# A two-layer decoder trunk on one core: output weights fetched two steps before they are split, and four pieces of work moved in the order

## The chip, the core and the metric

The kernel runs on one NeuronCore of a Trainium2 chip. The metric is device time of one launch in microseconds. PE is TensorE, DVE is VectorE, ACT is ScalarE, POOL is GpSimd, SP is SyncE, whose queue issues the DMAs.

## The reference, cut to what matters

```python
def mixer_sublayer(x, mem, w_in, w_mem_kv, w_out, main_fn):
    h = x @ w_in                       # columns [main | mem q | main gate | mem gate]
    y_main = main_fn(u_main)           # layer 0: causal pooling; layer 1: forgetting attention
    y_mem = memory_attention(q_mem, mem, w_mem_kv)      # 4 heads into 256 memory tokens
    y = concatenate([y_main * silu(g_main), y_mem * silu(g_mem)])
    return y @ w_out                   # then layer_norm(ALPHA * x + y)

def forgetting_attention(u, k, v, cum):                 # 16 heads of 64, causal
    logits = q @ k.T / 8 + cum[t] - cum[s]              # cum: running sum of log forget gates
    return softmax(logits) @ v
```

x is 1024 x 1024 in float32, there are two layers, and keys, values and forget gates of the second are projected once from the output of the first.

## The kernel before, in words

Every projection keeps float32 accuracy by splitting each operand into a rounded high part and a low remainder (`hi_lo`: ACT casts the high part, L142, DVE subtracts the low part, L143; `gp_hi_lo` does both on POOL, L146 and L147) and adding three products. A `slab` (L181) is one 128-column projection of all 1024 tokens: 48 matmuls with 512 columns each, two weight loads from `raw` buffers (three of them, shared by all weight loads), two evictions.

The order of PE is written out by hand. A `Fill` object holds generators of slab matmuls, and `pump(cols)` issues so many columns of them between the pieces of attention, so that PE has work while DVE and ACT do the softmax. DVE, ACT, POOL and SP are ordered by the scheduler.

**Memory attention** (`mem_attention`, once in each layer) loops over t = 0 to 9. For t < 8 `probs(t)` computes the logits of 128 tokens, their softmax (L283 to L294 on DVE and ACT) and a transposing DMA. At t = 3, 5, 7, 9 `values(c, h)` runs for four heads h; each is 12 matmuls into the only buffer of the tag O, taken out by DVE (L310). The fill is four gate slabs, spread evenly: one part behind the logits and one behind each h, at t = 9 three parts and then half parts.

**Start of the forgetting attention** (`start_units`): values and forget logits of the first heads (`v_first`), the first pair's keys and queries (`own`), a chain of small DVE operations for the forget gates, then their cumulative sum over tokens (L605 and L607 on PE), its transpose (L611), eight DMAs into `cumd` (L615) and the first loads of R, a row of `cumd` broadcast to all partitions (L670). `following` is the second pair's work: a key slab and a query slab.

**Forgetting attention** (`fox`): 8 pairs of heads, 16 steps in each pair (8 token tiles for each head, the longest first). A step computes the logits of one tile (L169 into the tag L, two buffers), DVE adds R and takes the minimum (L689), ACT exponentiates (L695) and scales (L712), DVE forms the remainder (L713), SP issues a transposing DMA (L722), and five steps later the values follow (L169 into O, evicted by L738 and L739). The pair's fill is spread evenly over its steps: three slabs (keys, queries, values) of the next pair, with evictions L627, L628, L638, L639 and, for the values, L651 and L236 to L244, and gate slabs of `gate_ahead` (L194, L195). Gates 0 and 1 run in pair 0, 2 in pair 2, 4 in pair 4, 7 in pair 7. Gates 3, 5 and 6 are late: their attention output goes to DRAM ungated, and in pair 7 `late_gate` reads it back into an R buffer, multiplies (L756, POOL) and writes it again; the others are multiplied in `pair_out` (L748, POOL).

**Output projection** (`OutProj`): W_out comes as 24 half tiles of 256 KB. `load` (L343) issues a transfer and the two split operations of `hi_lo` in one go, one half tile a step from the start of pair 7, eight in all; the rest follow in `rest`. `early` loads the memory part of y for the first 256 tokens and splits it, and its 48 matmuls fill the last five steps (L358).

Of the kernel before, what the change touches and what calls it, by code (L numbers as in the profile page):

```python
# [15 lines left out]
ALU = mybir.AluOpType  # L16
AX = mybir.AxisListType

P = 128
# [3 lines left out]
ST = S // P  # L23
# [48 lines left out]
def trunk_kernel(ctx, tc, x, xT, memT, win, wk, wv0, wv, wmk, wmv, wout, poolw, pscale, lng, lnb, bforget, out):  # L72
# [186 lines left out]
    def mem_attention(l, XH, XL, kv, qtile, ytile, yd):  # L259
# [52 lines left out]
        with tc.manual_schedule(engines={PE}):  # L312
            for t in range(ST + 2):
                part = fill.left / (5 * (ST + 2 - t))
                if t < ST:
                    probs(t)
                fill.pump(part if t <= ST else 3 * part)
                for h in range(MH):
                    if t >= 3 and t % 2 == 1:
                        values((t - 3) // 2, h)  # L320
                    fill.pump(part if t <= ST else part / 2)
            fill.pump(float("inf"))
        for h in range(MH):
            nc.vector.tensor_tensor(ys[h], ys[h], gs[h], ALU.mult)  # L324
# [2 lines left out]
    class OutProj:  # L327
# [2 lines left out]
        KKS = (4, 5, 0, 1, 2, 3)  # L330

        def __init__(self, l, wtile, yd):
            self.l, self.wtile, self.yd, self.ws, self.accs, self.n = l, wtile, yd, [{}, {}], None, 0

        def load(self, upto):

            for n in range(self.n, upto):
# [4 lines left out]
                r = raw([P, NH])  # L342
                nc.sync.dma_start(r, wout[self.l, nh, 2 * kk + j])  # L343
                hi_lo(h[j], lo[j], r)
            self.n = max(self.n, upto)

        def open(self, banks=(("pj", 3),) * 2 + (("L", 2),) * 2):
            accs = [ps([P, NH], *bank) for bank in banks]
# [12 lines left out]
                            )  # L361
                            yield NH

        def early(self, tiles):

            yh, yl = tiles
            for j in range(2):
                r, two = raw([P, 2, 2 * P]), slice(2 * j, 2 * j + 2)
                nc.sync.dma_start(r, self.yd[2, :, two, : 2 * P])
                hi_lo(yh[:, two, :], yl[:, two, :], r)  # L370

            def units():
                self.accs = self.open()
                yield from self.products(self.accs, 2, yh, yl)

            return units()

        def rest(self, resid, XH, XL, dst):
            self.load(24)
# [138 lines left out]
    with tc.tile_pool(name="in1", bufs=1) as in1:  # L518
# [135 lines left out]
        def start_units(own, following):  # L654

            yield from islice(own, 48)
            yield from v_first()
            gates = forget_gates()
            next(gates)
            for _ in v_turned():  # L660
                yield from islice(own, 6)
            yield from own
            next(gates)
            yield from islice(following, 9)
            next(gates)
            yield from islice(following, 39)

        def forget_rows(hd):
            R = sb([P, S], "R", 2, F32, in1)
# [1 line left out]
            return R  # L671

        def probs(hd, i, R, sums, behind):

# [77 lines left out]
        def late_gate(pr):  # L752
            o, g = sb([P, S], "R", 2, F32, in1), G()
            nc.sync.dma_start(o, y1d[pr // 4, :, pr % 4, :])
            yield from gate_units(win[1, 12 + pr], g, XH, XL)
            nc.gpsimd.tensor_tensor(o, o, g, ALU.mult)  # L756
            nc.sync.dma_start(y1d[pr // 4, :, pr % 4, :], o)

        def fox(following, out_proj):
# [8 lines left out]
            for hd in range(HEADS + 1):  # L768
# [3 lines left out]
                if hd < HEADS:  # L772
                    if b == 0:
                        o, sums = G(), sb([P, 4 * ST], "sums", 2, F32, small).rearrange("p (n b i) -> p n b i", n=2, b=2)
                        if 0 < pr < 7:
                            fill.add(pair_units(pr + 1), 3 * SLAB)
                        for ahead in {0: (0, 1), 2: (2,), 4: (4,), 7: (7,)}.get(pr, ()):
                            gate_ahead(ahead)
                        if pr == 0:
                            fill.add(following, SLAB)  # L780
                        for late in (3, 5, 6) if pr == 7 else ():
                            fill.add(late_gate(late), SLAB)
                    R, ahead_R = ahead_R, None
                for i in range(ST if hd < HEADS else LAG):
# [11 lines left out]
                        ahead_R = forget_rows(hd + 1)  # L796
                    if pr == 7:
                        step = b * ST + i
                        out_proj.load(min(step + 1, 6) if step < 9 else 8)
                        if step == 6:  # L800
                            lead = out_proj.early([xy((P, 4, 2 * P)) for _ in range(2)])
                    if hd < HEADS:
                        new = (hd, tile_of, o)
                        fresh[0] = probs(hd, tile_of, R, sums, behind)
# [85 lines left out]
```

## Time and profile before

| | us |
|---|---|
| three runs | 1282.02, 1282.96, 1287.71 |
| median | 1282.96 |
| profiled execution, its own time | 1289.07 |
| its span, first to last instruction | 1287.3 |
| PE busy / DVE / ACT / POOL | 1251.9 / 801.4 / 579.2 / 168.8 |
| mean granted TensorE clock | 0.993 |

A busy figure is the time in which an engine had an instruction under way; matmuls overlap, so a busy PE may still run slowly. Windows are stretches of the span, and a window's line gives each engine's busy time with the number of instructions, the granted clock (1.00 is full) and the DMA engines' busy share. In a timeline a bracket gives the idle time ahead of a group and what ended it. The profiled execution is one of several, and its times are some microseconds above the median's.

### The profile page before, as it was taken

To read this page: it belongs to the slowest core of one execution; us is meant where nothing else is said; L and a number is where in the kernel's file an instruction comes from. 1 tells how busy PE (TensorE), PEld (TensorE's weight loads), DVE (VectorE), ACT (ScalarE), POOL (GpSimd) and SP (SyncE) were. 2 spreads that over 40 slices of the span, in tenths; PEclk is the share of its full clock that TensorE was granted. 3 is DMA by queue.
4 is the path that set the end of the run, shared out by engine and by line. 5 is a ranking of instruction groups with operands and counts; after the bars stand their busy time and mean duration, and the time that the engine had idled before them with its cause. 6 is when DMAs were issued, how large, how long until landed. Compare 5 with 4: busy or idle time off the path is not lost. (4 is left out here: it accounts for less than half of the span.)

```text
span 1287.3 us, 19678 instructions
## 1 busy us (share of the span) xinstructions
PE 1251.9 (97%) x7018; PEld 1036.6 (81%) x7018; DVE 801.4 (62%) x1905; ACT 579.2 (45%) x1273; POOL 168.8 (13%) x267
## 2 busy tenths in 40 slices
PE   9999999999999999999999999999999999999997
PEld 7888878888778889887887788887888777788885
DVE  6452656355565457267456777777777887674644
ACT  5332642232331124265225667766766776653110
POOL 0000000000000000000003334333334231420000
PEclk9999999999999999999999999999999999999999
DMA  6351343212474226234516866868778786986430
GB/s 221 115 148 50 92 98 114 82 56 91 158 243 137 92 91 183 64 82 112 169 47 157 160 153 162 192 143 172 171 163 185 164 187 155 230 200 200 164 115 33
DMA packets 267426, 178.65 MB, mean 139 GB/s; under 512 B 212288, under 2 KB 225728, under 8 KB 267328
## 3 DMA queue, kind: packets, MB, share of 16 engines
q1 hardware_dynamic: 267328, 177.40, 52.0%
q8 instruction: 55, 0.90, 0.3%
q14 instruction: 43, 0.35, 0.1%
HBM read 94.97 MB, written 22.61 MB: 91 GB/s over the span
## 5 line engine op out<-in xcount | busy, mean ns | idle before, releaser
L181 PE MATMUL pj<-A,w 128*128 128x512 f32 x2928 | 726.5, 396 | 1.0 <-POOL w L147 0.6
L181 PEld LDWEIGHTS pj<-A,w 128*128 128x128 f32 x2928 | 539.5, 189 | 105.8 <-ACT A L142 1.8
L143 DVE TENSOR_TENSOR w<-raw,w 128x512 fp32r<-128x512 f32 x106 | 72.9, 689 | 117.0 <-ACT w L142 115.5
L142 ACT CAST w<-raw 128x512 fp32r<-128x512 f32 x106 | 65.6, 621 | 162.4 <-PE pj L181 103.7
L695 ACT ACTIVATE T<-MK,s 128x512 f32<-128x512 f32 x192 | 110.8, 577 | 56.6 <-DVE s L689 43.3
L713 DVE SCALAR_TENSOR_TENSOR P<-T,s,P 128x512 f16<-128x512 f32 x192 | 111.5, 613 | 34.5 <-ACT P L712 32.9
L712 ACT ACTIVATE P<-T,s 128x512 f16<-128x512 f32 x192 | 102.6, 576 | 48.2 <-issue 20.9
L169 PE MATMUL L<-B,B 128*128 128x512 f32 (+3 forms) x384 | 93.1, 346 | 13.9 <-DVE s L689 11.6
L169 PEld LDWEIGHTS L<-B,B 128*128 128x128 f32 x384 | 70.0, 188 | 36.2 <-DVE s L689 20.9
L689 DVE CUSTOM_DVE_ANT_0 MK<-L,R 128x512 f32<-128x512 f32 (+3 forms) x128 | 72.9, 570 | 15.9 <-PE L L169 10.7
L601 POOL MEMSET G<- 128x128 f32 x1 | 0.2, 205 | 620.3 <-DVE V L324 620.3
L169 PEld LDWEIGHTS <-V 128*128 128x128 f16 x1152 | 65.9, 99 | 17.9 <-issue 17.4
L169 PE MATMUL O<-T,V 128*128 128x128 f16 x1152 | 77.0, 222 | 0.0
L147 POOL TENSOR_TENSOR w<-raw,w 128x512 fp32r<-128x512 f32 x54 | 69.8, 1292 | 3.9
L142 ACT CAST T<-T 128x1024 fp32r<-128x1024 f32 x23 | 24.2, 1051 | 93.4 <-DMA T<-y1d 49.3
L682 POOL TENSOR_SCALAR_AFFINE_SELECT R<-R 128x128 f32<-128x128 f32 x128 | 40.4, 318 | 190.4 <-DVE s L689 107.7
L143 DVE TENSOR_TENSOR T<-T,T 128x1024 fp32r<-128x1024 f32 x23 | 28.1, 1220 | 58.1 <-PE L L358 41.6
L146 POOL TENSOR_SCALAR w<-raw 128x512 fp32r<-128x512 f32 x54 | 36.4, 675 | 143.6 <-PE pj L181 131.7
L213 PE MATMUL pj<-T,w 128*128 128x256 f32 x384 | 48.9, 285 | 2.7 <-ACT w L142 2.1
L213 PEld LDWEIGHTS pj<-T,w 128*128 128x128 f32 x384 | 46.9, 191 | 4.3 <-ACT w L142 2.8
L358 PE MATMUL pj<-B,T 128*128 128x512 f32 x186 | 46.5, 392 | 0.8 <-DVE B L143 0.8
L358 PE MATMUL L<-B,T 128*128 128x512 f32 x174 | 42.5, 389 | 0.0
(212 smaller groups left out, 1599.9 us busy)
## 6 DMA issues: line engine op xcount, KB each, us to landing
raw<-in_win_dram SPq DMA_DIRECT2D x96, 256.0 KB, 2.7
raw<-in_wout_dram SPq DMA_DIRECT2D x48, 256.0 KB, 3.3
B<-B SPq DMA_DIRECT2D x32, 256.0 KB, 3.9
R<-cumd SPq DMA_DIRECT2D x16, 512.0 KB, 4.3
y0d<-Y SPq DMA_DIRECT2D x12, 512.0 KB, 2.7
T<-y0d SPq DMA_DIRECT2D x12, 512.0 KB, 4.3
T<-y1d SPq DMA_DIRECT2D x11, 512.0 KB, 4.5
raw<-in_wmk_dram SPq DMA_DIRECT2D x16, 256.0 KB, 2.7
```

Source lines behind the costliest of these rows:

```text
L142: nc.scalar.copy(hi, src)
L143: nc.vector.tensor_tensor(lo, src, hi.bitcast(F32), ALU.subtract)
L147: nc.gpsimd.tensor_tensor(lo, src, hi.bitcast(F32), ALU.subtract)
L169: nc.tensor.matmul(acc, a, b, start=i == 0, stop=i == len(terms) - 1)
L181: nc.tensor.matmul(accs[n], a[:, k, :], b[:, kt, n * NH : (n + 1) * NH], start=kt == 0 and i == 0, stop=kt == KT - 1 and i == 2,)
L213: nc.tensor.matmul(acc, w[:, k, :], m[pc][:, k, :], start=pc == 0 and k == 0 and i == 0, stop=pc == 1 and k == 3 and i == 2,)
L358: nc.tensor.matmul(accs[a][nh], y[:, k, a * P : (a + 1) * P], w, start=kt == 8 and i == 0, stop=kt == 7 and i == 2,)
L682: nc.gpsimd.affine_select(R[:, qs], R[:, qs], [[-1, P]], ALU.is_ge, -NEG, base=0, channel_multiplier=1)
L689: nc.vector.tensor_tensor_reduce(p[:, lo:up], lg, R[:, lo:up], 1.0, top, ALU.add, ALU.min, m[:, n : n + 1])
L695: nc.scalar.activation(e, p[:, lo:up], AF.Exp, bias=top, scale=-1.0, accum_out=sums[:, n, hd % 2, i : i + 1],)
L712: nc.scalar.activation(pair[:, lo:up], e, AF.Copy, scale=r)
L713: nc.vector.scalar_tensor_tensor(pair[:, L + lo : L + up], e, r, pair[:, lo:up], ALU.mult, ALU.subtract)
```

## The change

Six edits in one:

- In `mem_attention`, at each t, three parts of the fill go behind the logits and half a part behind each head.
- `load` becomes `fetch`, which issues the transfer only, and `split`, which runs `hi_lo` on what was fetched. In pair 7, tile n is fetched in one step and split two steps later; the last two are split in steps 14 and 15.
- `early` becomes a generator whose two loads and two splits are issued in steps 7, 9, 10 and 12.
- In `start_units`, nine matmuls of `following` go ahead of the cumulative sum, and nine fewer go behind the transpose.
- In `fox`, gate 3 is filled in pair 3, no longer late; in pair 0 the rest of `following` (the second pair's queries) stands between gate 0 and gate 1.
- `late_gate` multiplies in four column pieces.

```diff
-                fill.pump(part if t <= ST else 3 * part)
+                fill.pump(3 * part)
                 for h in range(MH):
                     if t >= 3 and t % 2 == 1:
                         values((t - 3) // 2, h)
-                    fill.pump(part if t <= ST else part / 2)
+                    fill.pump(part / 2)
...
-        def load(self, upto):
+        def fetch(self, upto):
+            while self.n + len(self.raws) < upto:
+                n = self.n + len(self.raws)
+                r = raw([P, NH])
+                nc.sync.dma_start(r, wout[self.l, n // 2 % 2, 2 * self.KKS[n // 4] + n % 2])
+                self.raws.append(r)
+        def split(self, upto):
+            while self.n < upto:
+                self.fetch(self.n + 1)
...
+                hi_lo(h[j], lo[j], self.raws.pop(0))
+                self.n += 1
...
         def early(self, yh, yl):
             for j in range(2):
                 r, two = raw([P, 2, 2 * P]), slice(2 * j, 2 * j + 2)
                 nc.sync.dma_start(r, self.yd[2, :, two, : 2 * P])
+                yield
                 hi_lo(yh[:, two, :], yl[:, two, :], r)
+                yield
+            self.accs = self.open()
+            yield from self.products(self.accs, 2, yh, yl)
...
             yield from own
+            yield from islice(following, 9)
             next(gates)
             yield from islice(following, 9)
             next(gates)
-            yield from islice(following, 39)
+            yield from islice(following, 30)
...
-            nc.gpsimd.tensor_tensor(o, o, g, ALU.mult)
+            for c in range(4):
+                cols = slice(c * 2 * P, (c + 1) * 2 * P)
+                nc.gpsimd.tensor_tensor(o[:, cols], o[:, cols], g[:, cols], ALU.mult)
...
-                        for ahead in {0: (0, 1), 2: (2,), 4: (4,), 7: (7,)}.get(pr, ()):
+                        for ahead in {0: (0, 1), 2: (2,), 3: (3,), 4: (4,), 7: (7,)}.get(pr, ()):
                             gate_ahead(ahead)
-                        if pr == 0:
-                            fill.add(following, SLAB)
-                        for late in (3, 5, 6) if pr == 7 else ():
+                            if ahead == 0:
+                                fill.add(following, SLAB)
+                        for late in (5, 6) if pr == 7 else ():
                             fill.add(late_gate(late), SLAB)
...
-                        out_proj.load(min(step + 1, 6) if step < 9 else 8)
-                        if step == 6:
-                            lead = out_proj.early([xy((P, 4, 2 * P)) for _ in range(2)])
+                        if step == 7:
+                            lead = out_proj.early(*(xy((P, 4, 2 * P)) for _ in range(2)))
+                        if step in (7, 9, 10, 12):
+                            next(lead)
+                        out_proj.split(min(step - 1, 6) if step < 14 else step - 7)
+                        out_proj.fetch(min(step + 1, 6) if step < 12 else min(step - 5, 8))
```

More of the change, by code (lines that the diff above doesn't have):

```diff
@@ L332, in __init__ @@
         def __init__(self, l, wtile, yd):
-            self.l, self.wtile, self.yd, self.ws, self.accs, self.n = l, wtile, yd, [{}, {}], None, 0
-        def load(self, upto):
-            for n in range(self.n, upto):
+            self.l, self.wtile, self.yd, self.ws, self.accs = l, wtile, yd, [{}, {}], None
+            self.raws, self.n = [], 0
+        def fetch(self, upto):
[7 more added lines that the diff above has]
+                self.fetch(self.n + 1)
+                n = self.n
                 kk, nh, j = self.KKS[n // 4], n // 2 % 2, n % 2
@@ L341, in load @@
                 h, lo = self.ws[nh][kk]
[L342 to L345, printed above, removed]
+                hi_lo(h[j], lo[j], self.raws.pop(0))
+                self.n += 1
         def open(self, banks=(("pj", 3),) * 2 + (("L", 2),) * 2):
@@ L362, in products, with early @@
                             yield NH
-        def early(self, tiles):
-            yh, yl = tiles
+        def early(self, yh, yl):
             for j in range(2):
@@ L369, in early @@
                 nc.sync.dma_start(r, self.yd[2, :, two, : 2 * P])
+                yield
                 hi_lo(yh[:, two, :], yl[:, two, :], r)
[L372 to L376, printed above, removed]
+                yield
+            self.accs = self.open()
+            yield from self.products(self.accs, 2, yh, yl)
         def rest(self, resid, XH, XL, dst):
-            self.load(24)
+            self.split(24)
             gb = []
```

## The prediction

> **What bounds the kernel now.** I read the busy line of the page first, then the windows of the eight attention pairs, then the timeline of PE and DVE at each place where PE stood, and last the granted clock around those places.
>
> ```profile
> PE 1251.9 (97%) x7018; PEld 1036.6 (81%) x7018; DVE 801.4 (62%) x1905; ACT 579.2 (45%) x1273; POOL 168.8 (13%) x267
> ```
>
> PE is the bound: 1287.3 - 1251.9 leaves 35 us. No edit changes the number of matmuls, so only PE's waits, and what the waits bring with them, can move the time. A 512-column matmul follows the next one at 0.227 us (24 of L358 take 5.44 us in the chain).
>
> The next lines are windows from the first logits of a pair to those of the next: PE, PEld, DVE, ACT, POOL busy, PE clock, DMA.
>
> ```profile
> 736.20:790.30 54.10, 52.84 (x337) 42.87 (x338) 41.35 (x119) 37.31 (x89) 17.02 (x31) 0.97 0.68 162
> 790.30:851.50 61.20, 61.20 (x386) 50.86 (x385) 47.69 (x138) 41.55 (x95) 23.52 (x35) 1.00 0.76 173
> 851.50:907.00 55.50, 52.94 (x338) 42.67 (x336) 41.00 (x118) 37.22 (x89) 18.83 (x32) 0.97 0.75 161
> 907.00:968.20 61.20, 61.20 (x386) 50.87 (x385) 47.80 (x138) 41.54 (x95) 21.68 (x32) 1.00 0.74 167
> 968.20:1020.70 52.50, 51.30 (x337) 41.56 (x336) 40.87 (x118) 37.29 (x89) 18.84 (x32) 1.00 0.82 177
> 1073.70:1145.00 71.30, 66.12 (x386) 53.08 (x385) 49.85 (x140) 44.40 (x102) 23.49 (x32) 0.95 0.80 192
> ```
>
> Pairs 2 and 4 carry four slabs (192 matmuls of fill, 12 a step) and take 61.2 us without a PE gap. Pairs 1, 3, 5 carry three (9 a step) and show gaps. Pair 7 carries four and still takes 71.3. Every slab is 48 x 0.227 = 10.9 us.
>
> Four stretches of 3.41 us ran at half clock (0.50 below), each right behind a stretch of equal length in which PE was idle for 1.8 us or more. Two of the four, each with the stretch before it:
>
> ```profile
> 733.37:736.79 3.42, 1.62 (x8) 1.01 (x7) 2.93 (x9) 2.60 (x6) 2.09 (x3) 1.00 0.65 170
> 736.79:740.20 3.41, 3.41 (x16) 2.52 (x15) 2.15 (x5) 0.99 (x3) 0.59 (x2) 0.50 0.88 214
> 1119.08:1122.49 3.41, 0.96 (x5) 0.87 (x6) 1.95 (x4) 2.01 (x4) 1.27 (x3) 1.00 0.62 190
> 1122.49:1125.90 3.41, 3.41 (x20) 2.66 (x19) 1.49 (x7) 2.39 (x7) 1.53 (x2) 0.50 1.10 222
> ```
>
> Each costs PE 3.41 / 2 = 1.7 us. By PE start times the stretches ahead of the four held 2.0 to 2.5 us of idle; stretches with 1.8 us (at 607 and 669) brought none. So a wait of some 2 us costs 1.7 us more if it falls inside one stretch of this grid, about an even chance.
>
> **The change, part by part.**
>
> *Memory values, both layers.* The O bank has one buffer: value h+1 cannot start before DVE's L310 has taken value h out. Before, 4 matmuls of fill (0.91 us) stand between two values; after, at t = 3, 5, 7 only 2 (0.45), and the other 8 go ahead of the first value. At t = 9 both orders have 4.
>
> ```profile
> 177.15 1.17 PE L181 MATMUL pj<-A,w 128*128 128x512 f32 x4
> 178.17 0.84 PE L169 MATMUL O<-T,MK 128*128 128x128 f16 x12
> 178.82 1.17 PE L181 MATMUL pj<-A,w 128*128 128x512 f32 x4
> 181.71 0.83 PE L169 MATMUL O<-T,MK 128*128 128x128 f16 x12 [1.72 <-DVE Y L310]
> ```
> ```profile
> 177.38 0.49 DVE L310 TENSOR_SCALAR Y<-O,undo 128x256 f32<-128x256 f32 x1 [1.10 <-PE O L169]
> 179.60 1.67 DVE L294 SCALAR_TENSOR_TENSOR P<-P,s,P 128x256 f16<-128x256 f32 x4
> 181.19 0.48 DVE L310 TENSOR_SCALAR Y<-O,undo 128x256 f32<-128x256 f32 x1
> ```
>
> With DVE free, L310 ends 0.72 us after the value (177.15 to 177.87), and PE restarts 0.05 later: 0.77. Two matmuls and the 0.09 that a change of operand type costs cover 0.54. So each of 18 gaps (3 a step, 3 steps, 2 layers) waits 0.23 at least: 4.1. Now DVE's order. At t = 7 the second value's L310 moves behind L195, L143 and the four L294, which here end 7.05 us after the logits. The second value ends at 4.65 on that scale, so the third waits from 5.2 to 7.6 (2.4), with 0.2 each for its neighbours: 2.8 against 1.89 now. At t = 5 the second L310 stands behind one L294 and the third behind three: 0.25 + 0.7 + 0.4 = 1.3 against 0. At t = 3 the third stands behind all four: 0.25 + 0.25 + 0.8 = 1.3 against 0.76 (layer 0) and 0.50. Sum 2 x 5.4 = 10.8 after, 5.0 before: **+5.8 us**. Bounds: 4.1 - 5.0 = -0.9, if no eviction stands behind the softmax; +8, if two more wait out an L294 group.
>
> *Forget sums.* Nine matmuls of the second pair move ahead of the cumulative sum, which now waits 1.8 us for DVE:
>
> ```profile
> 671.79 0.46 PE L605 MATMUL O<-G,G 128*128 128x128 f32 x2 [1.65 <-DVE G L597]
> 687.89 0.73 PE L169 MATMUL L<-B,B 128*128 128x512 f32 x2
> ```
>
> 9 x 0.227 = 2.04 covers it. But the sum itself starts no earlier (DVE ends L597 at 671.64), and behind it stand a copy, a transpose, eight cumd DMAs (the last lands at 681.57), and the R load issued at 681.93, landing at 687.0; the first L689 starts at 687.14, on R. PE now arrives 1.7 us sooner and waits for R instead. One L628 (0.69) no longer stands between the first two L689. I take **-0.5** (from -1.8 to +0.3).
>
> *Second pair's queries ahead of gate 1.* The 1.97 us wait at 734 is PE on DVE's L639, the last of these queries. They are evicted in steps 9 to 11 of 16 instead; their two buffers were those of head 0 and are free by step 8. Gate 1's eviction, which then comes last, is wanted pairs later. **-2.0** (bound 0).
>
> *Fourth pair's gate in pair 3.* Pair 3 becomes a four-slab pair: 61.2 instead of 55.5 less 1.7 for a half-clock stretch = 53.8, so +7.4. Pair 7 becomes a three-slab pair; without its two stretches it took 67.9, and the three-slab pairs take 52.4, 53.8, 52.5, 53.0. It also splits 8 W_out and 2 y tiles (10 x 0.72 DVE = 7.2, against some 3 that its lack of key and value evictions saves), so I take 54.5: -13.4. Sum **-6.0** (pair 7 at 52.5: -8; at 57, all its stalls kept: -3.5). Gone too: the 512 KB load and store of the gate's R tile on SP, and 2.4 us of POOL (L756); four multiplies of 0.79 in pair 4 replace them, under POOL's 35% there.
>
> *W_out two steps ahead.* In pair 7 ACT waited 3.91 us for a W_out transfer with the softmax (L712) queued behind it, and PE 2.93. In the new order ACT's cast of that tile comes after those L712 and its DMA is issued one transpose sooner. At the pair's start the first two L689 now stand ahead of L244 and L143 on DVE, so the 1.67 wait there goes. Both are inside the 54.5. The raw pool keeps 3 buffers, so a fetched tile can hold up a win load on SP; I price that at 0, as two slabs' loads are 2.7 steps apart. L756 in four pieces: 0. The 127.8 us behind pair 7 have no PE gap, and the W_out loads that feed them keep their places: 0.
>
> *Sum of the waits:* 5.8 - 0.5 - 2.0 - 6.0 = -2.7. *Half clock:* the four stretches sat behind waits that the change removes (the pair 1 and pair 3 ones, two in pair 7): -6.8. New waits of 2 us or more are the two of 2.4 at t = 7 and the one for R: at even odds or a little above, with a remnant in pair 7, two come back: +3.4. By these rows the profiled execution goes from 1289.07 (span 1287.3) to 1289.1 - 2.7 - 3.4 = 1283.0. It lies 6.1 above the median, 1282.96. A run at another phase of the grid holds fewer than four: six waits of 1.8 to 2.0 us at nearly even odds and one of 2.9 at three in four make 3.4 on average. So I grant the median -2.7 - 2.4 = -5.1: **1277.9 us**, 0.4% down.
>
> **The rivals.** (1) DVE reaches the evictions as soon as values end: memory costs -0.9 instead of +5.8, and the two stretches at t = 7 go: 1277.9 - 6.7 - 2 = 1269. For it: at 160 to 166 four values passed with no wait. Against: DVE's order after. (2) The half-clock stretches hang on something other than these waits and stay: 1282.96 - 2.7 = 1280.3. For it: waits of 1.8 us brought none. Against: all four sit directly behind the four emptiest stretches. [...] (3) Slower: in pair 7, with 9 matmuls a step, ACT's W_out casts at the start of the last head (three of them, tiles 7 to 9) each wait for a transfer as the one at 1115 did, 2.93 on PE and 1.7 of half clock: three make 13.9, so 1291.8; with two the time is about as now. For it: tile 9's load waits for tile 7's split. (4) The early fetch does nothing, since three raw buffers pass it no slack: one such wait stays, 1277.9 + 4.6 = 1282.5.
>
> **How the numbers follow.** Chances: forecast 0.46, (1) 0.18, (2) 0.13, (3) 0.10, (4) 0.13. Half a percent, about what a measurement of this kernel can tell from no change, is 6.4 us: below 1276.5 or above 1289.4. The forecast's own range, 1273 to 1283, puts 0.18 of its 0.46 below. Faster 0.38 with (1) and a little of (2); slower 0.10; the rest 0.52. Range 1269 to 1289: it takes in (1), (2), (4) and leaves out most of (3).
>
> **What would show it.** Right: at t = 3, 5, 7 of both layers PE waits for L310 at nearly every value, some 2.4 at t = 7; no wait at the sum (L612 after) but one of 2 us ahead of the second logits; the pair 1 start without a wait; pair 3 near 61, pair 7 near 54. Wrong: no L310 waits, or pair 7 above 58, or as many half-clock stretches as before.

## The result and the profile after

| | before | after |
|---|---|---|
| median of six runs each, same chip (us) | 1283.13 | 1296.29 |
| lowest and highest | 1281.77 to 1287.71 | 1288.98 to 1296.76 |
| profiled execution: its own time, span | 1289.07, 1287.3 | 1293.36, 1291.6 |

The changed kernel is slower: the ratio is 1.0083, with a 95% interval of 1.0055 to 1.0111. The forecast was 1277.9 us with a range of 1269 to 1289; the measured time lies above both.

The profiled execution of after is one of its quicker ones, and that of before one of its slower ones, so the two spans are only 4.3 us apart. Stage lengths are read from the two profiles, prices of edits from the ratios of the timed runs.

A wait in the text runs from the start of one matmul to the start of the next, less the 0.227 us of a matmul; the bracket of a timeline goes by modelled ends and is some 0.2 us smaller. Lines of the source have moved in after: L358 of before is L367 there, L689 is L698, L712 and L713 are L721 and L722, L738 and L739 (ACT and DVE take a value out of the O bank) are L747 and L748, and L756 is L767. In an experiment's kernel they can differ again.

The busy line of the page first. PE's busy time has grown by 1.0 us with the same 7018 instructions; the rest of the loss is waiting.

```profile
PE 1252.9 (97%) x7018; PEld 1036.8 (80%) x7018; DVE 800.6 (62%) x1905; ACT 579.5 (45%) x1273; POOL 169.2 (13%) x276
```

Next, windows of after: pairs 1, 3 and 7, then the 13.6 us behind pair 7 up to the last attention value, then the rest of the output projection (the columns are those of the windows of before).

```profile
738.26:790.61 52.35, 51.22 (x337) 41.57 (x336) 41.31 (x121) 37.52 (x90) 18.88 (x32) 1.00 0.72 174
...
851.83:913.04 61.21, 61.21 (x386) 50.87 (x384) 44.89 (x129) 40.05 (x93) 23.05 (x36) 1.00 0.72 165
...
1080.27:1146.07 65.80, 57.00 (x338) 44.19 (x337) 47.09 (x133) 43.31 (x98) 17.59 (x30) 0.92 0.85 182
1146.07:1159.65 13.58, 12.17 (x84) 9.85 (x83) 7.87 (x17) 5.38 (x11) 4.70 (x6) 1.00 0.72 214
1159.65:1282.58 122.93, 121.54 (x538) 100.00 (x535) 61.14 (x106) 19.52 (x28) 1.73 (x2) 1.00 0.39 131
```

Pair 3 is the four-slab pair that was forecast (61.2). Pair 1 is shorter by 1.7 (54.1 before). Pair 7 has three slabs now (338 matmuls instead of 386) and takes 65.8 us where 54.5 was forecast; and the two stretches behind it, 12.0 and 121.0 us before, take 13.6 and 122.9.

In the memory stage, at t = 7 of layer 0, PE and then DVE (timelines, each line a group of like instructions; the bracket is the idle time ahead of it and what ended it):

```profile
178.36 0.71 PE L181 MATMUL pj<-A,w 128*128 128x512 f32 x2
181.33 1.13 PE L169 MATMUL O<-T,MK 128*128 128x128 f16 x12 [2.26 <-DVE Y L310]
```
```profile
179.21 1.67 DVE L294 SCALAR_TENSOR_TENSOR P<-P,s,P 128x256 f16<-128x256 f32 x4
180.80 0.48 DVE L310 TENSOR_SCALAR Y<-O,undo 128x256 f32<-128x256 f32 x1
```

Two matmuls between the values instead of four, the eviction (L310) behind four L294, and PE stands: this is the picture of the prediction. Ahead of the second logits PE meets the forget row instead of the forget sum, where the wait of 1.65 us is gone:

```profile
691.62 0.73 PE L169 MATMUL L<-B,B 128*128 128x512 f32 x2 [0.52 <-DVE s L698]
```

Now pair 7. PE's timeline at its two large waits:

```profile
1090.36 0.71 PE L181 MATMUL pj<-A,w 128*128 128x512 f32 x2
1094.03 2.15 PE L181 MATMUL pj<-A,w 128*128 128x512 f32 x3 [2.96 <-POOL w L146]
...
1127.07 2.24 PE L181 MATMUL pj<-A,w 128*128 128x512 f32 x9
1132.67 0.73 PE L169 MATMUL L<-B,B 128*128 128x512 f32 x2 [3.36 <-DVE s L698]
```

For the first one, POOL's and then SP's queue:

```profile
1093.36 0.62 POOL L146 TENSOR_SCALAR w<-raw 128x512 fp32r<-128x512 f32 x1 [4.28 <-DMA raw<-in_win_dram]
```
```profile
1090.03 0.53 SPq L151 DMA_DIRECT2D raw<-in_win_dram  x1
```

The fill of pair 7 is out of weights: its next `win` tile was issued only 9.8 us into the pair. Three W_out tiles, issued at 1040.1, 1061.0 and 1067.3 in pair 6 and not split to the end (L143) before 1088.9, held all three raw buffers across the pair's start. The kernel before has this too (its `win` tile comes 9.4 us into the pair), but there PE had stood at the softmax, behind L143 on DVE, for 1.67 us first, and came to the fill later: a wait of 0.80 us for POOL's L147 was what was left. For the second wait, ACT's queue:

```profile
1128.49 0.62 ACT L142 CAST B<-raw 128x512 fp32r<-128x512 f32 x1 [2.15 <-DMA raw<-in_wout_dram]
```

ACT stood at a W_out tile issued at 1125.92, which SP had reached at 1122.06 and could not issue before, its raw tile being taken; an eviction (L747), a gate's activation and two L721 were queued behind the cast, and PE's next logits behind those. Behind pair 7 the same happens once more, this time on DVE:

```profile
1157.41 1.39 DVE L143 TENSOR_TENSOR MK<-raw,MK 128x512 fp32r<-128x512 f32 x2 [4.34 <-ACT MK L142]
1158.83 0.49 DVE L748 SCALAR_TENSOR_TENSOR G<-O,unscale,G 64x256 f32<-64x256 f32 x1
```

L748 empties the one O bank, behind two W_out splits whose tiles came late; PE's last values waited 1.57 us for it, and its first y products 1.04 and 0.70 us more.

Half clock, the stretch around the wait at 1129 and the next one:

```profile
1130.60:1134.01 3.41, 1.34 (x6) 1.05 (x6) 3.12 (x10) 2.31 (x7) 1.70 (x3) 1.00 0.31 103
1134.01:1137.42 3.41, 3.41 (x14) 2.66 (x13) 2.20 (x6) 2.29 (x7) 0.29 (x1) 0.50 1.22 132
```

Between the first microseconds and the last, before and after both have four half-clock stretches: after has one in the memory stage (181.7) and three in pair 7, two of them in a row behind the wait at 1091.

### The profile page after: what moved, and what is told of

Read it like the earlier page. It is cut to its first block, busy times and chain, and to the rows that moved or that the text cites. A ratio compares the mean times of both kernels' runs of the same rounds, so it can differ in the third digit from the quotient of the medians.

```text
span 1291.6 us, 19675 instructions
## 1 busy us (share of the span) xinstructions
PE 1252.9 (97%) x7018; PEld 1036.8 (80%) x7018; DVE 800.6 (62%) x1905; ACT 579.5 (45%) x1273; POOL 169.2 (13%) x276
## 5 line engine op out<-in xcount | busy, mean ns | idle before, releaser
L181 PE MATMUL pj<-A,w 128*128 128x512 f32 x2928 | 726.0, 396 | 3.9 <-POOL w L146 3.0
L181 PEld LDWEIGHTS pj<-A,w 128*128 128x128 f32 x2928 | 538.8, 189 | 108.7 <-POOL w L146 3.4
L143 DVE TENSOR_TENSOR w<-raw,w 128x512 fp32r<-128x512 f32 x106 | 72.9, 689 | 115.6 <-ACT w L142 113.7
L722 DVE SCALAR_TENSOR_TENSOR P<-T,s,P 128x512 f16<-128x512 f32 x192 | 111.9, 613 | 29.5 <-ACT P L721 27.4
L721 ACT ACTIVATE P<-T,s 128x512 f16<-128x512 f32 x192 | 102.6, 575 | 41.4 <-issue 16.2
L698 DVE CUSTOM_DVE_ANT_0 MK<-L,R 128x512 f32<-128x512 f32 (+3 forms) x128 | 72.9, 569 | 25.1 <-PE L L169 18.2
L147 POOL TENSOR_TENSOR w<-raw,w 128x512 fp32r<-128x512 f32 x54 | 69.7, 1291 | 4.0
L143 DVE TENSOR_TENSOR T<-T,T 128x1024 fp32r<-128x1024 f32 x23 | 28.1, 1220 | 57.2 <-PE L L367 41.6
L367 PE MATMUL pj<-B,T 128*128 128x512 f32 x186 | 46.9, 392 | 2.1 <-ACT T L142 0.9
L287 ACT ACTIVATE P<-L,s 128x256 f32<-128x256 f32 x64 | 29.5, 473 | 31.6 <-DVE s L284 31.4
```

What stands on the lines that cost most here:

```text
L143: nc.vector.tensor_tensor(lo, src, hi.bitcast(F32), ALU.subtract)
L147: nc.gpsimd.tensor_tensor(lo, src, hi.bitcast(F32), ALU.subtract)
L181: nc.tensor.matmul(accs[n], a[:, k, :], b[:, kt, n * NH : (n + 1) * NH], start=kt == 0 and i == 0, stop=kt == KT - 1 and i == 2,)
L367: nc.tensor.matmul(accs[a][nh], y[:, k, a * P : (a + 1) * P], w, start=kt == 8 and i == 0, stop=kt == 7 and i == 2,)
L698: nc.vector.tensor_tensor_reduce(p[:, lo:up], lg, R[:, lo:up], 1.0, top, ALU.add, ALU.min, m[:, n : n + 1])
L721: nc.scalar.activation(pair[:, lo:up], e, AF.Copy, scale=r)
```

## The experiments

All kernels were timed in five rounds beside the kernel before on their chip; the kernel before had medians of 1284.9 to 1286.4 there, so ratios are compared, and 0.1% is 1.3 us. Three kinds of question: what each part costs alone, what is left when one part is taken out, and what pair 7 lacked.

**1. Memory values alone.**

```diff
-                fill.pump(part if t <= ST else 3 * part)
+                fill.pump(3 * part)
...
-                    fill.pump(part if t <= ST else part / 2)
+                    fill.pump(part / 2)
```

> The kernel before with one edit: memory values get half of their step's fill between them and the larger part ahead of the first one, as in the kernel after. Theory A (the loss is two independent losses, this one and pair 7's): the memory stages lengthen by 4.0 and 3.1 us as in the profile of after, so 1283 + 7 = 1290 us. Rival B (the whole loss of 13.3 us sits here, through half-clock stretches that the new waits call up): 1295 us or more. Rival C (the waits for L310 are paid back by the pairs, which start later and find their loads ready): 1283 to 1285 us.

Measured: 1291.3 us, ratio 1.0039 (1.0026 to 1.0052), so +5.0 us. Theory A. Its larger waits for L310 are those of after: 0.79, 0.61, 0.40, 2.43 us in each layer. All of them together grow from 5.2 us in before to 11.0 over both layers.

**2. The fourth pair's gate in its own pair, alone.**

```diff
-{0: (0, 1), 2: (2,), 4: (4,), 7: (7,)}
+{0: (0, 1), 2: (2,), 3: (3,), 4: (4,), 7: (7,)}
...
-                        for late in (3, 5, 6) if pr == 7 else ():
+                        for late in (5, 6) if pr == 7 else ():
```

> The kernel before with one edit: the fourth pair's gate is filled into its own pair instead of into pair 7; W_out is loaded and split as before, the three raw buffers are free between. Theory A (pair 7 of after is long because the early W_out tiles hold the raw buffers and the gate weights come late): pair 3 takes 61.2 instead of 55.5 (+5.7), pair 7 some 55 to 58 instead of 71.1 (-13 to -16), so 1283 - 9 = 1274 us. Rival D (pair 7 is long because nine matmuls of fill a step leave PE waiting on DVE and ACT, whatever the loads do): pair 7 stays near 65.8 as in after and the time is 1283 + 5.7 - 5.3 = 1283 us.

Measured: 1287.9 us, ratio 1.0017 (1.0006 to 1.0028), +2.2 us. Neither theory in its size: nearly the whole gain is missing, without any early fetch. Windows of pair 7 and of the stretch behind the last value:

```profile
1082.00:1143.81 61.81, 54.20 (x338) 42.34 (x336) 45.94 (x133) 42.98 (x98) 18.82 (x27) 0.97 0.79 191
...
1155.84:1279.59 123.75, 121.54 (x538) 100.03 (x535) 62.49 (x108) 19.59 (x29) 1.24 (x1) 1.00 0.40 134
```

Pair 7 loses 9.3 us for 10.9 us of matmuls taken out, and the output projection gives 2.8 back (waits of 1.86 and 0.69 us at its first y products). PE's waits in pair 7 are 2.46, 0.37, 0.96, 0.42, 0.80, 1.53 and 2.11, together 8.6 us, plus one half-clock stretch: its 51.5 us without them became 61.8. The stage lengths of this profile and that of before add to about nothing; the +2.2 is that of the timed runs.

The largest wait stands where before had its 1.67 us: the softmax behind the last value eviction (L244) and the split of a W_out tile (L143) on DVE. The last one stands where before had its 2.93 us: ACT waits for a W_out transfer with the softmax queued behind it. The 0.80 us is for a `win` tile and the 1.53 us for a transposed tile of the softmax; the other three are for the softmax on DVE. PE at both, then DVE ahead of the first and ACT ahead of the last:

```profile
1088.72 0.73 PE L169 MATMUL L<-B,B 128*128 128x512 f32 x2 [2.29 <-DVE s L689]
...
1127.43 1.31 PE L169 MATMUL L<-B,B 128*128 128x384 f32 x4 [1.95 <-DVE s L689]
```
```profile
1087.28 0.78 DVE L143 TENSOR_TENSOR MK<-raw,MK 128x512 fp32r<-128x512 f32 x1
```
```profile
1123.49 0.62 ACT L142 CAST B<-raw 128x512 fp32r<-128x512 f32 x1 [3.31 <-DMA raw<-in_wout_dram]
```

**3. W_out two steps ahead, alone** (`fetch` and `split`, and `early` as a generator; pair 7 keeps four slabs).

```diff
-                        out_proj.load(min(step + 1, 6) if step < 9 else 8)
+                        out_proj.split(min(step - 1, 6) if step < 14 else step - 7)
+                        out_proj.fetch(min(step + 1, 6) if step < 12 else min(step - 5, 8))
```

> The kernel before with one edit: W_out tiles are fetched two steps ahead of their splits, and the y tiles two steps ahead of theirs; pair 7 keeps four slabs. Theory A (early tiles hold the raw buffers, gate weights come late): pair 7, with three late gates that load win tiles, gets new waits at L181 of 3 us and more in its first and last head: 75 us or more instead of 71.1, so 1287 us or more. Rival D (the number of matmuls a step decides, the fetch is free or a gain): pair 7 loses its 3.9 us wait for W_out with ACT, 67 us, so 1279 us.

Measured: 1287.3 us, ratio 1.0007 (0.9997 to 1.0017): nothing, or up to 2 us of loss. The wait at L181 that theory A expected is there, 4.12 us from 1083 on, and the one with ACT in the last head is down from 2.93 to 1.06 and 0.86: the early fetch trades one wait for another, and pair 7 stays at 71.2, not at the 75 of theory A.

**4. The two moves of the order, alone.**

```diff
             yield from own
+            yield from islice(following, 9)
             next(gates)
...
                             gate_ahead(ahead)
-                        if pr == 0:
-                            fill.add(following, SLAB)
+                            if ahead == 0:
+                                fill.add(following, SLAB)
```

> The kernel before with one edit: nine matmuls of the second pair ahead of the forget sums, and the second pair's queries ahead of the second gate. Theory A: the waits of 1.8 us at the sum and 1.97 us at the start of pair 1 go, one of about 0.7 us before the second pair's logits comes, and the half-clock stretch in pair 1 goes with its wait (1.7): 1283 - 5 = 1278 us. Rival C (pairs lose what the stage before them gained, since their loads set the pace): 1283 us.

Measured: 1283.2 us, ratio 0.9975 (0.9962 to 0.9987), -3.2 us. Theory A, less than its 5: in the profile the wait before the second pair of logits is 2.35 us, not 0.7, and brings a half-clock stretch of its own; pair 1 starts without a wait and takes 52.4.

The four parts add to +0.38%, 4.9 us; the whole change is +0.83%, 10.7 us. So parts meet, if the multiply in four pieces, which was not timed alone, costs nothing.

**5 and 6. The gate and W_out together, and the change without W_out.**

> The kernel before with two edits: the fourth pair's gate in its own pair, and W_out and y tiles fetched two steps ahead. Alone they measured +2.2 and +0.9 us. Theory A (they meet in pair 7: with nine matmuls of fill a step the win tiles that wait for a raw buffer are late): pair 7 near 66 instead of 61.8, and 1285 + 3 + 6 = 1294 us. Rival (they only add): 1288 us.

Measured: 1292.2 us, ratio 1.0053 (1.0033 to 1.0073), where the two alone add to 1.0024. The early fetch costs 0.07% with four slabs and 0.36% with three. Its pair 7 shows the waits of after, one by one (3.04 us at L181, 1.58, 0.79, 3.64 us). Against the gate alone, the third and the fifth `win` tile issued in the pair come 3 us later in it (27.1 and 39.3 us into the pair, 24.1 and 36.5 there), and two half-clock stretches in the pair stand against one. Pair 7 takes 64.1 us.

> The kernel after, with W_out loaded and split in one step as before (and the y tiles loaded and split in one step). The parts alone measured +5.0 (memory values), +2.2 (gate in its own pair), +0.9 (W_out) and -3.2 (order) on top of 1285.3; they add to +4.9, and the whole change measured 0.83%, 10.7. Theory A (the missing 5.8 is the early W_out tiles meeting a pair 7 that has only nine matmuls a step to cover them): pair 7 takes about 62 as with the gate moved alone instead of 65.8, and the time is 1285 + 5.0 + 2.2 - 3.2 = 1289 us. Rival E (the missing part comes from the memory stage or the order meeting another edit): pair 7 stays near 65 or the time near 1295 us.

Measured: 1290.9 us, ratio 1.0036 (1.0020 to 1.0051); pair 7 takes 61.7. Theory A: inside the change W_out costs 0.47%, 6 us. Gate and W_out together (+0.53%), memory (+0.39%) and order (-0.25%) add to +0.67% of the 0.83%, and the rest is inside the intervals.

**7. The change without the memory edit** (experiment 1 taken back in the kernel after).

> The kernel after with the fill of the memory values spread as before. Theory A: it takes back what the memory edit cost alone, 5.0 us, and nothing in the pairs changes: 1296 - 5 = 1291 us, still above the kernel before. Rival E (the memory edit shifts the pairs' loads and so makes part of pair 7's loss): 1287 us or less, pair 7 below 64 us.

Measured: 1288.1 us, ratio 1.0013 (0.9999 to 1.0027). Pair 7 is 66.3, so rival E's mechanism is not there; the step of 0.70% is above the 0.39% of the edit alone, but their intervals meet.

**8. The change with a fourth raw buffer.** Room for it (2 KB a partition) comes from two small tiles.

```diff
-        return sb(list(shape), "raw", 3)
+        return sb(list(shape), "raw", 4)
...
-        undo = small.tile([P, 64], F32, tag="undo", ...
+        undo = small.tile([P, 4], F32, tag="undo", ...
...
-small.tile([P, 8], F32, tag="edge", name="edge")
+small.tile([P, 8], F32, tag="edge", name="edge", bufs=1)
```

> The kernel after with four raw buffers instead of three (2 KB a partition, found by shrinking two small tiles; nothing else differs). Theory A (early W_out tiles hold raw buffers and the gate's win tiles come late): the wait of 3.1 us at L181 at the start of pair 7 goes, pair 7 takes 62 us or less instead of 65.8, and the time is 1290 us or less. Rival F (the win loads are late because SP issues them behind the value transposes and W_out, whatever the number of buffers): pair 7 and the time stay, 1295 us.

Measured: 1292.6 us, ratio 1.0046 (1.0031 to 1.0061). Pair 7 falls to 56.1 us, 1.6 above the forecast's 54.5: the wait of 3.13 us at L181 is gone, and pair 6 issues two `win` tiles ahead instead of one, the second 14 us before pair 7 starts. So it was buffers, not SP's order. But the stretches behind grow from 13.6 and 122.9 to 14.6 and 129.8:

```profile
1083.98:1140.07 56.09, 52.04 (x338) 41.31 (x336) 44.88 (x129) 42.03 (x96) 18.41 (x28) 1.00 0.85 200
...
1154.70:1284.48 129.78, 125.92 (x537) 100.95 (x535) 61.68 (x106) 18.46 (x27) 2.23 (x2) 0.99 0.37 123
```
```profile
1153.16 0.69 DVE L143 TENSOR_TENSOR MK<-raw,MK 128x512 fp32r<-128x512 f32 x1 [4.16 <-ACT MK L142]
1153.88 0.49 DVE L748 SCALAR_TENSOR_TENSOR G<-O,unscale,G 64x256 f32<-64x256 f32 x1
```

A shorter pair 7 comes to the sixteen W_out splits of the output projection before their transfers have landed. DVE waits 4.16 us at one of them with L748 behind it, and PE waits 2.59, 1.39 and 2.80 us, with a half-clock stretch at 1163. A second loss in this run has nothing to do with it: the matmuls of both output projections follow each other at 0.2335 us instead of 0.227 wherever W_out lies in one of the big tiles, some four in five of them.

**9. The same with the W_out pool moved by 32 bytes.**

```diff
+    nc.vector.memset(const.tile([P, 8], F32, name="shift"), 0.0)
```

> The kernel after with four raw buffers, and one unused tile of 32 bytes a partition ahead of the pools, so that the pool with the W_out tiles begins at 128 KB exactly instead of 32 bytes below it. In the last run with four buffers, output projection matmuls whose W_out tile lay in that pool followed each other at 0.2335 us instead of 0.227, in both layers, which is about 2 x 2.9 us. Theory G (the address of the moving operand does it): the spacing is 0.227 again and the time 1292.6 - 5.8 = 1287 us, pair 7 still near 56. Rival H (the fourth buffer's extra transfers do it): spacing and time stay, 1292 us.

Measured: 1296.9 us, ratio 1.0083 (1.0063 to 1.0103). The spacing is still 0.2335 and theory G falls in this form. Pair 7 is 56.9. That 32 bytes made it 0.37% slower than experiment 8 is not explained (see the pad of 1760 bytes below).

**10. The last one with the first y tile ahead of the W_out tiles.**

```diff
+            first = self.y_tile(0, 0) if self.accs else None
             self.split(24)
...
-                src, yh, yl = T([P, 4, 2 * P], F32), ...
+                yh, yl = first or self.y_tile(sp, c)
```

> The kernel before last, with the first y tile of the output projection loaded and split ahead of the last sixteen W_out tiles instead of behind them. With four buffers pair 7 fell to 56.1, but the stretch behind it grew from 134.5 to 144.4 us. Theory I (DVE and ACT split sixteen W_out tiles first, and PE comes to the y tile earlier than they do): the waits of 1.4 and 2.8 us before the first y products go, with their half-clock stretch: 1287 - 5 = 1282 us. Rival J (the stores of the late gates' pairs set the end): PE waits as long elsewhere in the tail, 1287 us.

Measured: 1288.5 us, ratio 1.0029 (1.0017 to 1.0041). The waits of 2 to 3 us behind pair 7 are gone (0.60 and 0.70 are left), and so is the half-clock stretch. Against experiment 9 this is 0.54%, against experiment 8 0.17%, whose program differs from that of 9 by 32 bytes alone; so the size is uncertain, the place is not.

**11. The same edit in the kernel after, with three buffers.**

> The kernel after with one edit: the first y tile of the output projection loaded and split ahead of the last W_out tiles. Theory I: pair 7 stays at 65 to 66 us, the waits of 1.04 and 0.70 us before the first y products and perhaps the 1.57 us at L748 go: 1296 - 3 = 1293 us. Rival (with three buffers the tail is held by the raw tiles, not by their order): no gain, 1296 us.

Measured: 1296.6 us, ratio 1.0087 (1.0069 to 1.0106): no gain, the rival. The wait moves: DVE now stands at the y tile with the value's eviction (L754 in this kernel) behind it, and PE waits 2.75 us there instead of 1.57, 1.04 and 0.70 at three places.

```profile
1158.76 1.23 DVE L143 TENSOR_TENSOR T<-T,T 128x1024 fp32r<-128x1024 f32 x1 [5.39 <-ACT T L142]
1160.02 0.49 DVE L754 SCALAR_TENSOR_TENSOR G<-O,unscale,G 64x256 f32<-64x256 f32 x1
```

**12. What the slower matmuls are: the kernel before with its pools moved by 1760 bytes, and a candidate with the tiles at their old distance.**

```diff
+    nc.vector.memset(const.tile([P, 440], F32, name="shift"), 0.0)
```

> The kernel before with one unused tile of 1760 bytes a partition, so that the pool with the W_out tiles begins at 128 KB exactly; no instruction of the program differs but the tile's memset. Theory G: the output projections are already at 0.227 us a matmul, nothing to gain there: 1286 us. If the address also sets the 0.231 us of the matmuls inside the attention pairs (some 2000 of them), 1286 - 7 = 1279 us.

Measured: 1293.7 us, ratio 1.0052 (1.0034 to 1.0070), expected by neither. The output projections are at 0.227 with the W_out pool at the same address as in experiment 9, so that address does not slow the matmul. The loss is in PE's waits (pair 7 74.0 instead of 71.1, and 20.5 us at half clock from 673 on instead of 13.7) in a program that differs by one memset; what in the addresses does it stays open.

The candidate is the change without the memory edit and the four-piece multiply, with four buffers and the first y tile ahead, first with the pool as in experiment 9:

> The kernel after without its memory edit and without its four-piece multiply, with four raw buffers, the pool at 128 KB and the first y tile ahead of the W_out tiles: everything in the change that the runs so far found good, with what it lacked. Theories A, G and I together: 1282 - 9 = 1273 us, below the kernel before (1286 on the last chip) and below the one with the order alone. If J holds instead of I: 1278 us.

Measured: 1280.5 us, ratio 0.9967 (0.9955 to 0.9979), with the slow spacing. Then with the spare bytes taken ahead of the pools:

```diff
-    invc = const.tile([P, 16], F32, name="invc")
+    invc = small.tile([P, 16], F32, tag="c_invc", name="invc", bufs=1)
```

(and `psc`, `pschalf`, `edge` in the same way, with an unused tile of 32 bytes among the small ones)

> The candidate with its spare bytes taken from the constants ahead of the pools instead of from the small tiles behind them, so that W_out tiles and y tiles lie as far from each other as in the kernel before (with a fourth buffer so far they lay 320 or 288 bytes closer). Theory K (a matmul is slower when its moving operand and the weights being loaded lie at certain distances): 0.227 us a matmul again in both output projections, and 1280.5 - 5.7 = 1275 us. Rival L (it is the fourth buffer, wherever it lies): 0.2335 us and 1280 us.

Measured: 1279.2 us, ratio 0.9955 (0.9938 to 0.9972), the fastest of all. Like groups of output projection matmuls of experiment 8 and of this one (the last two figures ahead of the bar are total busy time in us and the mean of one in ns):

```profile
L367 PE MATMUL L<-B,T 128*128 128x512 f32 x48 | 12.5, 394 | 0.0
```
```profile
L368 PE MATMUL L<-B,T 128*128 128x512 f32 x54 | 13.7, 389 | 0.0
```

389 ns is the mean of before, and the spacing is 0.227 again, with four buffers: rival L falls. Whether it is the distance of W_out and y tiles (320 or 288 bytes less in the slow runs, from the sizes of the tiles) or the y tile's own address, these runs do not part.

Its windows of pair 7 and of the output projection:

```profile
1078.68:1137.54 58.86, 53.79 (x337) 42.59 (x336) 45.91 (x133) 42.77 (x98) 17.95 (x25) 0.97 0.90 194
...
1149.58:1271.48 121.90, 121.37 (x537) 100.00 (x535) 61.04 (x106) 19.42 (x28) 0.74 (x1) 1.00 0.40 133
```

**13. What of the candidate is needed:** without the early W_out and with three buffers (the gate, the order, the y tile); with four buffers and the order alone; with four buffers, the gate, the order and the y tile. The last two have the tiles at their old distance.

> The kernel before with the fourth pair's gate in its own pair, the two moves of the order, and the first y tile ahead of the last W_out tiles; three buffers, W_out loaded with its split. If the 2.8 us that the tail lost with the gate moved are the y tile's place: 1285 + 2.2 - 3.2 - 2.8 = 1281 us, tail back to 121 us. If they are something else: 1284 us.

> The kernel before with the two moves of the order and four raw buffers at the old distance of W_out and y tiles; gate and W_out as before. If the gate's move and the early W_out gain something once there is a buffer: pair 7 near 71, 1283 us against 1279 for the candidate. If the fourth buffer alone does it: 1279 us or less.

> The candidate with W_out loaded in the step of its split, as before. If the early W_out is worth the wait for its transfer in pair 7 (2.9 us in the kernel before) and half a half-clock stretch: pair 7 some 61 instead of 58.9, 1282 us. If four buffers make the early fetch needless: 1279 us.

Measured: 1283.1 us, ratio 0.9977 (0.9963 to 0.9992); 1285.1 us, 1.0000 (0.9985 to 1.0016); 1282.4 us, 0.9968 (0.9953 to 0.9983). In the first, the stretches behind pair 7 take 12.0 and 122.2 us with a single wait of 0.70 us, against 12.0 and 123.8 in experiment 2: with W_out loaded with its split, the y tile's place helps on three buffers too, though not all the way to 121 us.

The fourth buffer alone gains nothing. With it, the gate in its own pair and the y tile gain 0.32% (last against middle), with pair 7 at 60.6 instead of 73.2. On three buffers the same two edits add nothing to the order's moves (0.9977 against 0.9975 in experiment 4). But the two kernels with the gate stand nearly alike, 0.9977 and 0.9968, and so do their pairs 7, 60.1 and 60.6 us; what differs is the kernel with four buffers and the order alone, which came out slower than the order alone on three (the intervals just touch) and has its tiles at other addresses. So it is not shown that the gate needs the fourth buffer. The early W_out then takes pair 7 to 58.9, and its 0.13% of the time lies inside the intervals.

One more, the kernel before with the order's moves, early W_out and the four buffers of experiment 8, gave less than was expected:

> The kernel before with the two moves of the order, W_out and y tiles fetched two steps ahead, and four raw buffers; memory values and the fourth pair's gate as before. Theory A: with a buffer to spare the early fetch takes away the 2.9 us wait for ACT's W_out transfer in pair 7 and its half-clock stretch, and the waits for win tiles do not grow: 1285 - 3.2 - 4 = 1278 us. Rival F (SP's order of issue sets the lateness): no better than the order's moves alone, 1282 us or more.

Measured: 1286.1 us, ratio 0.9991 (0.9976 to 1.0007). Pair 7 is 70.9. The slow spacing costs it 2.8 us in the last output projection (123.8 instead of 121.0), and as much again in the first. Its wait for win tiles is gone, but one of 3.2 us for the softmax stands in its place.

## Why the prediction was wrong, step by step

**Memory values: right.** +5.8 was forecast and +5.0 (3.3 to 6.7) measured alone. At t = 7 the wait is 2.43 us, as in the sum, and all waits for L310 come to 11.0 us over both layers where the sum had 10.8. This was not luck: the terms hold step by step.

**Forget sums and second pair's queries: right in kind, near in size.** -2.5 and the half-clock stretch of pair 1 were forecast, -3.2 measured. The wait for the forget row came as said, 0.68 us in after, but 2.35 in experiment 4.

**Fourth pair's gate, first failed step: "so I take 54.5: -13.4".** Pair 3 came out at 61.2 as forecast. Pair 7 did not: alone, the move takes it to 61.8. The working took nearly the whole of the pair's waiting away with the slab, because the other three-slab pairs take 52.4 to 53.8. But the fill did not make these waits. With its matmuls out, PE waits 8.6 us and loses one half-clock stretch (experiment 2), against 6.1 us and two stretches before, at the same two places and some more: behind the W_out split at the pair's start, and for ACT's W_out transfer in the last head. Such a pair should have been priced at its old length less the matmuls: 71.2 - 10.9 = 60.3, from the rows already shown. Alone, the gate's move was to bring -6.0 and measured +2.2; pair 7 is 7.3 us longer than forecast and the stretch behind it 2.8, which is more than the difference.

**W_out, second failed step: "The raw pool keeps 3 buffers, so a fetched tile can hold up a win load on SP; I price that at 0".** The mechanism was named and mispriced. With four slabs to cover it the price is 0.9 us, with three it is 4.6 us (experiment 5 against 2, 0.36%), and inside the change 6 us, with wide intervals on each. Pair 7 with three slabs, over the thirteen profiles that have it so (they differ in the other edits too), shows the mechanism:

| pair 7 (us) | W_out loaded with its split | fetched two steps earlier |
|---|---|---|
| three raw buffers | 60.1 to 61.8 | 64.1 to 66.3 |
| four raw buffers | 60.6 | 56.1 to 58.9 |

Early tiles cost where they take a buffer from the `win` loads, and gain where they do not; a buffer without early tiles does nothing, in the one run of it. The kernels with four buffers have other addresses too; the short pair 7 stands at all three placings that were run. At the pair's start the forecast was right that the 1.67 us wait would go; it did not ask what PE would meet next, which was the `win` tile, 3.13 us. Rival 3 had the place right: casts for W_out that wait for a transfer with the softmax behind, in the last head. It was one of them, 3.5 us, and not three; the rest of the loss lies at the start of the pair and behind it.

**Third failed step: the tail priced at 0**, since it has "no PE gap" and its loads "keep their places". They kept their places in the queue, but pair 7 had been their cover. Made shorter, it hands its waits on: +2.8 us in experiment 2, +3.5 in after, +11.4 in experiment 8 (of which 2.9 are the slow spacing); in the kernels whose pair 7 keeps four slabs the tail is as before, the slow spacing aside. With W_out fetched early on three buffers the y tile's place alone does not help (experiment 11). Loaded with its split, it leaves 1.2 us of the 2.8 (experiment 13), and with four buffers 0.7 to 1.5 are left, the slow spacing taken off (experiments 10, 12 and 13).

**Half clock.** Two of four stretches were to come back; the profile of after has four again, so the -3.4 of the sum did not come. One sits where it was expected, behind L310 at t = 7. The three in pair 7 sit behind waits that the forecast had only as "a remnant". The rows of before were also read a little wrong: ahead of the stretch at 1081.5 the idle time is 3.41 - 1.71 = 1.70 us, not "1.8 us or more"; counted by matmul starts it is 2.2.

Together, in us: memory +5.0, order -3.2, gate +2.2, W_out alone +0.9, and 3.7 for gate and W_out meeting, from 0.53% less 0.24%. That is 8.6 of the 10.7 us measured; the whole change has an interval of 3.6 to either side, so no further cause is needed, and none is excluded, the four-piece multiply among them.

## What to carry to other kernels

Before an engine's work is taken out of a stage, ask of each wait in it whether that work makes it or hides it. Here, with a slab taken out of pair 7 (experiment 2), the waits stayed, 8.6 us against 6.1 before, and the stage behind lost the cover of the longer one, 2.8 us. Fetching earlier out of a fixed pool of buffers takes a buffer from somebody for as long as it is early: in pair 7 with three slabs it cost 2 to 6 us on three buffers and gained 1.7 to 4.5 on four, while the fourth buffer alone did nothing there. In the time of the whole kernel that gain is 0.13%, inside the intervals. So an early fetch and the buffer for it are one edit, to be tried together, and with them the load that the next stage meets first.

## What the runs showed of the hardware

**The half clock followed the idle time of one stretch, not one gap.** The clock's records of before and after run in multiples of 3.413 us. On that grid, with a matmul counted as 0.227 us from its start, and without the first 20 us and what follows the last matmul, the eight half-clock stretches of before and after came behind stretches with 2.04 to 2.52 us of PE idle, in one wait or several; every other stretch of the two held 1.81 us or less. Over the profiles of before, after and all experiments: of stretches with 2.1 us or more all 45 were followed by a stretch at half clock; with 1.9 to 2.1 us 13 of 38; with 1.5 to 1.9 us 2 of 76. Thirteen single gaps of 2.4 to 3.6 us were followed by none: each lay across two stretches. In after, two waits of 2.43 us for L310 at t = 7 show both: the one from 178.90 lay inside one stretch, with half clock behind it at 181.70; the one from 610.55 lay across the border at 611.78, and none came. (By the busy column of a window, whose ends are modelled, the idle time ahead of the four of before comes out 0.0 to 0.5 us lower.)

**The spacing of matmuls differed between programs that differ in addresses alone.** 0.2267 us or 0.2335 us a 512-column matmul, for some four in five matmuls of both output projections. Between the two candidates of experiment 12 only addresses differ, and the mean of one matmul of the group L<-B,T is 394 ns in the first and 389 ns in the second; with four buffers the slow spacing shows in experiments 8 to 10, the first candidate and the last run of experiment 13, and not in the second candidate and the two runs with its placing. Which address, or which distance, is open.

**A pad of 1760 bytes, and nothing else, cost 0.52%** (run of the kernel before, 1293.7 against 1284.9 us). Runs that change the size of a tile therefore carry an unknown of this order; experiments 1 to 7 and the two with the y tile on three buffers change no tile's size.
